# The split weights of an encoder trunk moved to other byte offsets

## The chip, the core and the metric

The kernel runs on one core of one Trainium2 chip. The time is device microseconds of one execution; the median of three runs is given, and one more execution was recorded by the hardware profiler. TensorE (PE in the profile) multiplies, with its weight loads shown as an engine of their own (PEld); VectorE is DVE, ScalarE ACT, GpSimd POOL, and SyncE (SP) issues most DMAs.

## What is computed

Two layers of an encoder on 256 tokens of width 1024, in float32, and a last RMSNorm:

```
def hybrid_layer(x, ...):
    h = rms_norm(x, g_mix)
    b_a, c_a, x_a, u_p, q, k, v, ga, gp, gt = jnp.split(h @ w_in, split_points(), axis=-1)
    y_a = short_conv_mixer(b_a, c_a, x_a, conv_w, w_a_out)
    y_p = multiscale_pool_mixer(u_p, w_pool, pool_scale)
    y_t = windowed_gqa(q, k, v, rel_bias, sink) @ w_attn_out
    merged = sigmoid(ga) * y_a + sigmoid(gp) * y_p + sigmoid(gt) * y_t
    x = x + merged @ w_o
    gate, up = jnp.split(rms_norm(x, g_ffn) @ w_gu, [D_FF], axis=-1)
    return x + (silu(gate) * up) @ w_down
```

The weights of both layers are read once, about 170 MB; each 128x128 block of them is used for all 256 tokens.

## The kernel before

Activations lie with channels on the 128 partitions and tokens along the free dimension. Every float32 product is made of three reduced-precision ones: a value is split into a high part (`hi` for weights, the first half of a pair for activations) and a remainder (`lo`, the second half). `mm3` issues the three matmuls of a block: high weight by high activation (L166), high weight by low activation (L167), low weight by high activation (L168). Each has a 128x128 block of weights as the stationary operand, which a weight load brings in, and 256 columns of an activation as the moving one. The only products with the operands the other way round are those of the last layer's down projection (`down_nat`, L626 to L628): there the activation `fa` is stationary and 512 columns of weights stream.

`plan_layer` writes out the order in which blocks are used, and the host lays the blocks out in that order in `wst`. A chunk of 16 blocks (1 MB) is one DMA into one of three `raw` tiles. `convert` splits half a chunk, 8 blocks: ScalarE casts it to `hi` (L139) and VectorE subtracts (`lo`, L140). `advance`, called from `take` whenever a half chunk is begun, converts three half chunks ahead. `hi` and `lo` are tags with five buffers each in the pool `wp`, so the sixth half chunk overwrites the first.

Beside these blocks TensorE computes the attention scores (`sc`, L356 and L357, stationary `q`, moving `kk`), transposes the probabilities (`pt`, L385), multiplies them with the values (`o`, L400, stationary `vt`), and sums squares for the norms. `norm_rows` and the transposes of `x` (`xt`, L684) are a few matmuls more.

Pools place their tiles one after another in each partition. The constants come first, then `wp`, then `act`, which begins with the tile `x`, then `tmp`. The tile `x` holds 96 numbers of parameters and 112 unused ones ahead of the activations:

```
NG = L * 6 * KT + 112
xc = act.tile([P, NG + KT * T], F32, name="x")
```

All tiles that hold split activations are 2048 bytes long and follow each other (`xg`, `z` and `m`; `q`, `ao` and `fa`; `h`; `pp`), and both halves of a pair are 1024 bytes, so that all begin at one place within 512 bytes. The same holds for the blocks in `hi` and `lo`.

Of the kernel before, what the change touches and what calls it, by code (L numbers as in the profile page):

```python
# [9 lines left out]
F32R = mybir.dt.float32r  # L10
# [6 lines left out]
P = 128  # L17
# [7 lines left out]
NEG = -1e30  # L25
CB, CC, CX, CU, CQ, CK, CV, CGA, CGP, CGT = 0, 8, 16, 24, 32, 40, 42, 44, 52, 60
CT = 16
HT = 8

HEADS = []  # L30
# [5 lines left out]
def plan_layer(last):  # L36

    out = []

    def inner(mat, ns, nk=KT):  # L40
        for n in ns:
            for k in range(nk):
                out.append((mat, k, n))

    def outer(mat, ns, nk=KT):
        for k in range(nk):
            for n in ns:
                out.append((mat, k, n))

    outer("in", (CK, CK + 1, CV, CV + 1))  # L50
    for q in range(2):
        inner("in", [CQ + 4 * q + j for j in range(4)])
    inner("in", [CGA + n for n in range(8)])
    for n in range(8):
        inner("in", (CC + n, CX + n, CB + n))
    inner("in", (CU, CU + 1))
    inner("a", range(8))
    for n in range(8):
        inner("in", (CGP + n, CGT + n))
        if n % 2 == 1 and n < 7:  # L60
            inner("in", (CU + n + 1, CU + n + 2))
        inner("t", (n,))
        out.extend(("pool", k, n) for k in range(2))
        if n >= 2:
            out.extend(("o", n - 2, m) for m in range(8))
    for j in range(4):
        out.extend(("o", k, m) for k in (6, 7) for m in (2 * j, 2 * j + 1))
    for q in range(NQ):
        ns = (2 * q, 2 * q + 1, FT + 2 * q, FT + 2 * q + 1)
        if q == 0:  # L70
            outer("gu", ns)
        else:
            inner("gu", ns)
        if q >= 1:
            for k in (2 * q - 2, 2 * q - 1):
                out.extend(("down", k, m) for m in range(8))
    ks = (2 * NQ - 2, 2 * NQ - 1)
    if last:
        for k in ks:
            out.extend(("down", k, m) for m in range(8))  # L80
    else:
        for j in range(4):
            out.extend(("down", k, m) for k in ks for m in (2 * j, 2 * j + 1))
    return out


NCH = len(plan_layer(False)) * L // CT

# [4 lines left out]
def trunk(ctx, tc, wst, xT, sinkb, rb, invc, gfin, ident_d, out):  # L93
# [5 lines left out]
    wp = ctx.enter_context(tc.tile_pool(name="wp", bufs=3))  # L99
# [2 lines left out]
    psA = ctx.enter_context(tc.tile_pool(name="psA", bufs=4, space=PSUM))  # L102
    psB = ctx.enter_context(tc.tile_pool(name="psB", bufs=4, space=PSUM))

    uid = [0]

    def nm(s):
# [10 lines left out]
    def dma_chunk(c):  # L118
        raw = wp.tile([P, CT * P], F32, name=f"raw{c}", tag="raw", bufs=3)
        if c < 2:  # L120
            for a, b, xa, xb in (((0, 4, 0, 1), (4, 8, 1, 2), (8, 16, 2, 4)), ((0, 8, 4, 6), (8, 16, 6, 8)))[c]:
                s = slice(0 if xa == 0 else NG + xa * T, NG + xb * T)
                if xa == 0:
                    nc.sync.dma_start(xc[:, s], xT[:, s])
                nc.sync.dma_start(raw[:, a * P:b * P], wst[c, :, a * P:b * P])
                if xa > 0:
                    nc.sync.dma_start(xc[:, s], xT[:, s])
        else:
            nc.sync.dma_start(raw, wst[c])
        raws[c] = raw  # L130

    def convert(hc):
        c = hc // 2
        raw = raws[c][:, (hc % 2) * HT * P:(hc % 2 + 1) * HT * P]
        hi = wp.tile([P, HT * P], F32R, name=f"hi{hc}", tag="hi", bufs=5)
        lo = wp.tile([P, HT * P], F32R, name=f"lo{hc}", tag="lo", bufs=5)
        for a, b in (((0, 4), (4, 8)) if hc < 2 else ((0, 8),)):
            s = slice(a * P, b * P)
            S.activation(hi[:, s], raw[:, s], AF.Copy)  # L139
            V.tensor_tensor(lo[:, s], raw[:, s], hi[:, s].bitcast(F32), op=ALU.subtract)  # L140
        his[hc], los[hc] = hi, lo

    def advance(pos):
        while state["dma"] < NCH and state["dma"] * CT <= pos + 3 * CT - 1:
            dma_chunk(state["dma"])
            state["dma"] += 1
        while state["cv"] < 2 * NCH and state["cv"] * HT <= pos + 3 * HT:
            convert(state["cv"])
            state["cv"] += 1

    def take(key, width=1):
        pos = state["pos"]
        if pos % HT == 0:
            advance(pos)
        for i in range(width):
            l, mat, k, n = plan[pos + i]
            assert (l, mat, k, n) == (key[0], key[1], key[2], key[3] + i), (plan[pos + i], key)
        hc, j = pos // HT, pos % HT
        assert j + width <= HT
# [544 lines left out]
    for j in range(4):  # L704
        convert(j)
        xg_tiles(0, 0, j, st)
# [141 lines left out]
```

## Time and profile before

| | |
|---|---|
| median of 3 runs | 960.26 us (959.83 to 961.04) |
| the profiled execution | 965.28 us |
| its span, first to last instruction | 963.1 us |
| granted TensorE clock | 0.999 |
| matmuls, weight loads | 7881, 7881 |
| moved by DMA | 178.17 MB, mean 185 GB/s |

The span is what the profile shows; some 2 us of the execution lie outside it. Busy time of TensorE adds up overlapping matmuls only once, so a busy share near 100% tells that it never stood still, not how fast it went. The views used below are the page's list of engines and its chain of work, the groups by line (count, busy us, mean ns of one, idle time ahead of them), the timeline of one engine (start, duration) and the table of stretches.

### The profile page before, as it was taken

Reading aid. Unit: us, or ns where it says so; the run is one execution under the profiler, and the core shown is the slowest. Engines: PE = TensorE matmul, PEld = TensorE weight load, DVE = VectorE, ACT = ScalarE, POOL = GpSimd, SP = SyncE. Lnnn points to the kernel's source line nnn. Section 1 sums busy time; section 2 is a strip of 40 time slices with the busy share of each in tenths; the row PEclk is TensorE's granted clock in tenths of the full one; section 3 lists DMA queues with packets and bytes.
Section 4 is the critical chain, followed back from the end, with each engine's and each line's share of the span. In section 5 each row is a group of like instructions: output and inputs, shape, how many; then the busy total and the mean of one; then the engine's idle time right before and its main releaser. Section 6 shows DMA issues by size and latency. Waiting matters only on the chain.

```text
span 963.1 us, 19117 instructions
## 1 busy us (share of the span) xinstructions
PE 952.8 (99%) x7881; PEld 939.9 (98%) x7881; DVE 711.3 (74%) x1277; ACT 551.0 (57%) x916; POOL 38.8 (4%) x60
## 2 busy tenths in 40 slices
PE   8999999999999999999999999999999999999997
PEld 8999999999999999999999999999999999999996
DVE  7999998577679955545599998975677698555555
ACT  6866777655456644444477666765545575444444
POOL 5000000000001000000020000000000020000000
PEclk9999999999999999999999999999999999999999
DMA  8656545544554555555543745444555455655541
GB/s 300 251 186 210 202 162 173 198 176 176 203 191 174 178 190 200 179 177 194 197 178 132 246 166 185 148 171 175 181 197 192 176 190 182 218 176 187 197 142 44
DMA packets 26967, 178.17 MB, mean 185 GB/s; under 512 B 3136, under 2 KB 3664, under 8 KB 6656
## 3 DMA queue, kind: packets, MB, share of 16 engines
q1 hardware_dynamic: 24768, 169.99, 49.8%
q0 software_dynamic: 2112, 6.97, 2.5%
q8 instruction: 61, 1.00, 0.4%
q14 instruction: 26, 0.21, 0.1%
HBM read 175.86 MB, written 1.08 MB: 184 GB/s over the span
## 4 chain that ended last, share of the span: by engine, by line
PE 98%; DMA 1%; DVE 0%; ACT 0%; SPq 0%; issue 0%
PE b L167 25%; PE b L166 25%; PE b L168 25%; PE dn L166 2%; PE dn L168 2%; PE dn L167 2%; PE dn L628 2%; PE dn L627 2%; PE dn L626 2%; PE wo L167 2%; PE wo L166 2%; PE o L400 2%; PE wo L168 2%; PE pt L385 1%; PE sc L357 1%; PE sc L356 1%
## 5 line engine op out<-in xcount | busy, mean ns | idle before, releaser
L140 DVE TENSOR_TENSOR lo<-raw,hi 128x1024 fp32r<-128x1024 f32 (+1 forms) x322 | 389.5, 1218 | 200.9 <-ACT hi L139 199.9
L139 ACT ACTIVATE hi<-raw 128x1024 fp32r<-128x1024 f32 (+1 forms) x322 | 335.9, 1051 | 308.4 <-PE b L167 189.7
L166 PE MATMUL b<-h,hi 128*128 128x256 f32 x1344 | 377.4, 281 | 0.0
L168 PE MATMUL b<-h,lo 128*128 128x256 f32 x1344 | 376.0, 280 | 0.0
L167 PE MATMUL b<-h,hi 128*128 128x256 f32 x1344 | 376.0, 280 | 0.0
L166 PEld LDWEIGHTS b<-h,hi 128*128 128x128 f32 x1344 | 255.0, 190 | 0.2
L168 PEld LDWEIGHTS b<-h,lo 128*128 128x128 f32 x1344 | 253.9, 189 | 0.0
L167 PEld LDWEIGHTS b<-h,hi 128*128 128x128 f32 x1344 | 252.4, 188 | 0.2
L166 PE MATMUL b<-xg,hi 128*128 128x256 f32 x448 | 125.2, 280 | 0.9 <-DVE xg L253 0.9
L167 PE MATMUL b<-xg,hi 128*128 128x256 f32 x448 | 124.9, 279 | 0.9 <-DVE xg L256 0.9
L168 PE MATMUL b<-xg,lo 128*128 128x256 f32 x448 | 124.7, 278 | 0.2 <-DVE lo L140 0.2
L167 PEld LDWEIGHTS b<-xg,hi 128*128 128x128 f32 x448 | 84.2, 188 | 1.3 <-DVE xg L256 1.3
L166 PEld LDWEIGHTS b<-xg,hi 128*128 128x128 f32 x448 | 84.2, 188 | 1.1 <-ACT hi L139 1.0
L168 PEld LDWEIGHTS b<-xg,lo 128*128 128x128 f32 x448 | 84.6, 189 | 0.4 <-DVE lo L140 0.4
L166 PE MATMUL dn<-fa,hi 128*128 128x256 f32 x176 | 49.5, 281 | 0.0
L167 PE MATMUL dn<-fa,hi 128*128 128x256 f32 x176 | 49.5, 281 | 0.0
L168 PE MATMUL dn<-fa,lo 128*128 128x256 f32 x176 | 49.5, 281 | 0.0
L369 ACT ACTIVATE s<-s,sm 128x256 f32<-128x256 f32 x64 | 31.7, 497 | 17.5 <-DVE sm L364 17.5
L166 PE MATMUL b<-z,hi 128*128 128x256 f32 x128 | 36.3, 284 | 0.0
L168 PE MATMUL b<-z,lo 128*128 128x256 f32 x128 | 36.0, 281 | 0.0
L166 PE MATMUL b<-ao,hi 128*128 128x256 f32 x128 | 36.0, 281 | 0.0
L167 PE MATMUL b<-ao,hi 128*128 128x256 f32 x128 | 36.0, 281 | 0.0
(176 smaller groups left out, 1494.1 us busy)
## 6 DMA issues: line engine op xcount, KB each, us to landing
raw<-wst SPq DMA_DIRECT2D x158, 1024.0 KB, 4.9
bias<-stab POOLq DMA_DIRECT2D x16, 384.0 KB, 4.5
raw<-wst SPq DMA_DIRECT2D x3, 512.0 KB, 8.0
out<-yg SPq DMA_DIRECT2D x4, 256.0 KB, 2.2
x<-xT SPq DMA_DIRECT2D x3, 256.0 KB, 8.0
raw<-wst SPq DMA_DIRECT2D x2, 256.0 KB, 5.1
gf<-gfin POOLq DMA_DIRECT2D x2, 256.0 KB, 3.1
x<-xT SPq DMA_DIRECT2D x1, 232.0 KB, 2.7
```

The costliest lines, as they stand in the source:

```text
L139: S.activation(hi[:, s], raw[:, s], AF.Copy)
L140: V.tensor_tensor(lo[:, s], raw[:, s], hi[:, s].bitcast(F32), op=ALU.subtract)
L166: PE.matmul(dst, wh, xh, start=start, stop=False, skip_group_check=skip)
L167: PE.matmul(dst, wh, xl, start=False, stop=False, skip_group_check=skip)
L168: last_mm[0] = PE.matmul(dst, wl, xh, start=False, stop=stop, skip_group_check=skip)
L356: PE.matmul(ps[:, half(j)], qs[t][j][:, cs], kh, start=True, stop=False)
L357: PE.matmul(ps[:, half(j)], qs[t][j][:, cs], kl, start=False, stop=True)
L369: S.activation(ss[i // 2][:, i % 2], ss[i // 2][:, i % 2], AF.Exp, bias=sm[:, 4 + i:5 + i], accum_out=sm[:, 12 + i:13 + i])
L400: PE.matmul(ps[:, half(j)], vv, pts[kt][i][:, half(j)], start=(kt == i == 0), stop=(kt == i == 1))
L626: PE.matmul(d, ah[:, cs], wh, start=(k == 0), stop=False)
L627: PE.matmul(d, ah[:, cs], wl, start=False, stop=False)
L628: PE.matmul(d, al[:, cs], wh, start=False, stop=(k == FT - 1))
```

## The change

The ten buffers `hi` and `lo` become slices of one tile, `split_w`. A slot is 4096 bytes as before, five for `hi` and then five for `lo`, reused in the same rotation; the first begins 5 elements, or 20 bytes, into the tile. The tile has 8 elements, or 32 bytes, more than the ten slots need.

```
 CT = 16
+HB, WOFF = 5, 5
 HT = 8
...
+    split_w = wp.tile([P, 2 * HB * HT * P + 8], F32R, name="split_w", bufs=1)
...
     raw = raws[c][:, (hc % 2) * HT * P:(hc % 2 + 1) * HT * P]
-    hi = wp.tile([P, HT * P], F32R, name=f"hi{hc}", tag="hi", bufs=5)
-    lo = wp.tile([P, HT * P], F32R, name=f"lo{hc}", tag="lo", bufs=5)
+    hi, lo = [split_w[:, i + WOFF:i + WOFF + HT * P]
+              for i in (hc % HB * HT * P, (HB + hc % HB) * HT * P)]
```

The two programs have the same instructions in the same order on every engine, with the same waits. They differ in addresses. In bytes within a partition, modulo 512:

| | before | changed |
|---|---|---|
| `raw` | 224 | 256 |
| split weights | 224 | 244 |
| split activations | 160 | 192 |
| weights minus activations, 7,152 matmuls (L166 to L168) | 64 | 52 |
| the same for 264 matmuls with the operands exchanged (L626 to L628) | 448 | 460 |
| `q` minus `kk`, scores (L356, L357) | 128 | 128 |
| `vt` minus probabilities (L400) | 0 | 0 |
| probabilities minus `ident`, transposes (L385) | 320 | 352 |

In each row with a minus, the stationary operand's place stands first and the moving one's is taken off. `raw` now lies behind the split weights, since the one tile is allocated first.

## The prediction

> **What bounds the kernel.** I read the page first: busy time, then the chain that ended last.
>
> ```profile
> PE 952.8 (99%) x7881; PEld 939.9 (98%) x7881; DVE 711.3 (74%) x1277; ACT 551.0 (57%) x916; POOL 38.8 (4%) x60
> PE 98%; DMA 1%; DVE 0%; ACT 0%; SPq 0%; issue 0%
> ```
>
> TensorE holds 98% of the chain. So what counts is the step from the start of one matmul to the start of the next, which no view prints: the duration of one matmul, some 0.28 us, overlaps the next two. I take the step from the timeline of TensorE, where the first column is the start in microseconds, at two places.
>
> ```profile
> 499.73 0.28 PE L168 MATMUL b<-xg,lo 128*128 128x256 f32 x1
> 499.84 0.28 PE L166 MATMUL b<-xg,hi 128*128 128x256 f32 x1
> ...
> 501.43 0.28 PE L168 MATMUL b<-xg,lo 128*128 128x256 f32 x1
> 399.76 0.28 PE L167 MATMUL b<-h,hi 128*128 128x256 f32 x1
> 399.88 0.28 PE L168 MATMUL b<-h,lo 128*128 128x256 f32 x1
> ...
> 401.41 0.28 PE L166 MATMUL b<-h,hi 128*128 128x256 f32 x1
> ```
>
> From 499.73 to 501.43 lie 15 steps: 113.3 ns each. From 399.76 to 401.41 lie 14: 117.9 ns. These are the same instructions, 256 columns against a split weight tile, with the same places of operands within 512 bytes, and neither piece has an idle TensorE. **There are two paces, and they last.** The table of stretches shows how long (us, then busy time and matmuls of each engine, granted clock in the column after POOL):
>
> ```profile
> 33.00:57.00 24.00, 24.00 (x214) 24.00 (x213) 23.37 (x49) 18.81 (x35) 0.00 (x0) 1.00 0.38 134
> 180.00:291.00 111.00, 111.00 (x945) 111.00 (x944) 75.86 (x125) 58.56 (x82) 0.00 (x0) 1.00 0.52 181
> 311.50:494.00 182.50, 182.50 (x1552) 182.50 (x1552) 116.49 (x142) 88.84 (x119) 5.67 (x4) 1.00 0.52 183
> 507.00:531.00 24.00, 24.00 (x214) 24.00 (x213) 23.44 (x48) 17.50 (x32) 0.00 (x0) 1.00 0.39 133
> ```
>
> A row also counts the two or three matmuls that cross its edges, about 2.4. So 24.00 / 211.6 = 113.4 ns in the first and last, and 182.50 / 1549.6 = 117.8 ns in the third. The clock is 1.00 in all four, so it isn't the throttle. How many matmuls go at each pace can be read from their durations, which differ too (the groups of 34 to 56 us, then of 182 to 290 us, then of the whole run):
>
> ```profile
> L167 PE MATMUL b<-xg,hi 128*128 128x256 f32 x65 | 17.9, 276 | 0.0
> L167 PE MATMUL b<-h,hi 128*128 128x256 f32 x176 | 49.5, 281 | 0.0
> L167 PE MATMUL b<-h,hi 128*128 128x256 f32 x1344 | 376.0, 280 | 0.0
> L168 PE MATMUL b<-xg,lo 128*128 128x256 f32 x448 | 124.7, 278 | 0.2 <-DVE lo L140 0.2
> ```
>
> Fast is 276 ns, slow 281 ns. 376.0 us / 1344 = 279.8 ns, so a quarter of the h matmuls are fast; 124.7 / 448 = 278.3 ns, so half of the xg matmuls are; z, ao, m and fa stand at 281. That makes 4032 / 4 + 1344 / 2, about 1,700 of 7,152. Counting the starts of all 7,152 one by one gives 1,841 steps of 112 to 115 ns, 5,231 of 116 to 119 ns, and 80 beside a wait or a change of operand. I use these.
>
> **The change, part by part.** The number, order, waits and sizes of instructions stay, and so do 10 slots of 1024 weights with the same reuse. What changes is where bytes lie. (1) The split weights begin at byte 244 of 512 instead of 224. (2) Everything allocated behind them moves up by 32 bytes, so the activations begin at 192 instead of 160. (3) The distance from activation to weight becomes 52 bytes instead of 64 for the 7,152 matmuls, and 460 instead of 448 for the 264 of 512 columns. (4) Distances that don't involve the split weights stay: 128 for the scores, 0 for the value products. What (1) to (3) do to the pace is the whole question, and this trace holds distances 64, 448, 128 and 0 only. Rows of the last two, and of the shortest step in the trace, the transposes (the row of the chain gives 8 in 0.87 us):
>
> ```profile
> 83.15 0.28 PE L356 MATMUL sc<-kk,q 128*128 128x256 f32 x1
> ...
> 84.11 0.27 PE L385 MATMUL pt<-ident,s 128*128 128x128 f32 x1
> 76.54 0.28 PE L400 MATMUL o<-ph,vt 128*128 128x256 f32 x1
> ...
> 77.50 0.28 PE L166 MATMUL b<-h,hi 128*128 128x256 f32 x1
> 70.36 0.87 PE pt L385 x8
> ```
>
> Eight steps each: 0.96 / 8 = 120 ns at distance 128, 0.96 / 8 = 120 ns at distance 0, and 0.87 / 8 = 109 ns for a transpose, which streams half the columns and takes a whole weight load, so that the load is likely to pace it. So 109 ns is the nearest thing to a **floor**, distances 0 and 128 cost 11 ns over it, and distance 64 costs 4.5 or 9. The good place lies between 0 and 128, and 52 is inside. That is the argument for a gain. It is not a proof, since a straight line from 0 to 64 would put 52 about 0.4 to 1.3 ns above the two paces of 64.
>
> Terms, against the profiled execution (965.28 us, of which 963.1 are span; the median of three is 960.26, half a per cent less, so I take differences):
> - Slow steps that become fast: 5,231 x (117.8 - 113.35) = 23.3 us. If instead fast ones become slow: 1,841 x 4.45 = 8.2 us lost.
> - 264 matmuls of 512 columns. From 810.40 to 811.54 in the timeline lie five steps:
>
> ```profile
> 810.40 0.39 PE L626 MATMUL dn<-hi,fa 128*128 128x512 f32 x1
> ...
> 811.54 0.39 PE L628 MATMUL dn<-hi,fa 128*128 128x512 f32 x1
> ```
>
> That is 228 ns, 10 over twice the 109; at distance 460 anything from -10 to +10 ns, so -2.6 to +2.6 us. I take 0, since the place moves least in proportion.
> - Writes of the split weights that start off a 32-byte boundary. VectorE has such a pair in the convolution:
>
> ```profile
> L506 DVE SCALAR_TENSOR_TENSOR y<-c,x,y 128x255 f32<-128x255 f32 x16 | 7.7, 480 | 1.7 <-ACT y L505 1.2
> L507 DVE SCALAR_TENSOR_TENSOR y<-c,x,y 128x255 f32<-128x255 f32 x16 | 7.7, 478 | 0.1
> L139 ACT ACTIVATE hi<-raw 128x1024 fp32r<-128x1024 f32 x318 | 333.5, 1057 | 302.8 <-PE b L167 189.7 <-PE dn L167 30.4 <-PE dn L628 26.9
> ```
>
> L506 writes 4 bytes in, L507 at the tile's start: 480 and 478 ns, so nothing. For ScalarE no row shows it. It may lose or gain; its 318 casts of 1057 ns have 302.8 us of idle time ahead of them, most of it waiting for TensorE to free a slot, and that time is the cover. Only if each became over half longer would the attention stretches run out of it. I take 0.
> - What is late next if TensorE speeds up: VectorE, busy 23.37 of 24.00 us in the first stretch above, and 23.44 of 24.00 in the last. Both are fast already, so the forecast isn't capped; at 109 ns the same 211 matmuls take 23.1 us, and VectorE would hold each stretch back by about 0.3 us.
>
> Sum: 960.26 - 23.3 = **937 us**.
>
> The Trainium skill, "TensorE: Matmul & The Clock Gate", Part 2, step 1, says that TensorE reads the streamed operand and the weights through two independent ports, so that a weight load takes no read bandwidth from the running matmul. By that rule the place of one against the other changes nothing, and the sum is 960; the paces of 113.4, 117.8 and 120 ns for one shape at one clock don't rule it out, but leave nothing else in sight that differs.
>
> **The rivals.**
> - *Slower: the load gets longer.* In the slow stretch one weight load in three takes longer than the others, in the fast one none does (groups of 182 to 290, then of 34 to 56 us):
>
> ```profile
> L166 PEld LDWEIGHTS b<-h,hi 128*128 128x128 f32 x176 | 33.8, 192 | 0.0
> L167 PEld LDWEIGHTS b<-h,hi 128*128 128x128 f32 x176 | 33.0, 188 | 0.0
> L166 PEld LDWEIGHTS b<-xg,hi 128*128 128x128 f32 x65 | 12.2, 188 | 0.0
> ```
>
> A slot that begins 20 bytes in no longer starts on a 32-byte boundary. If that adds 4 ns to a load, and the load's end starts the next matmul, the fast pace becomes about 117.4 and nothing else gains: all 7,072 steps near 117.8, 960.26 + 8.2 = 968. It decides from the point where a load is longer than the 113.4 ns step leaves room for. For it: fast and slow differ by one such 4 ns. Against: the long load may be an effect of the slow pace. The Trainium skill, "SBUF — State Buffer", the note on cachelines, says that memory is read in 16-byte lines and that each crossing into a new one pays a penalty; 512 bytes that start 4 bytes into a line touch 33 of them instead of 32. No run here shows a load at such a place.
> - *Slower, toward distance 0.* If 52 behaves as 0 does, all go to 120 ns: 5,231 x 2.2 + 1,841 x 6.65 = 23.8 us, 984. For it: it's a step in that direction. Against: 52 is nearer to 64.
> - *Faster still.* If the two streams no longer meet at all, the steps reach the 109 ns: 5,231 x 8.8 + 1,841 x 4.35 = 54 us, 906. For it: the transposes show that a load can follow a load every 109 ns. Against: no 256-column matmul in the trace runs so.
> - *Nothing.* If the distance isn't what sets the pace (a pace that was only picked up at a wait or at a transpose would be the same whatever the place), both paces stay in their shares: 960. Against: steps at 0 and 128 are slower from their first to their last.
>
> **How the numbers follow.** Nearly all steps at the fast pace, 930 to 945: 0.36, the likeliest, because the fast pace is one that this kernel already holds for 24 us on end and 52 stays inside the good side. Partly so, 945 to 958: 0.08. Toward the floor, below 930: 0.20, a quarter of it below 905. No change, within 0.2% (which is about what a measurement of this kernel can tell): 0.08. All slow or a longer load, 963 to 970: 0.16. Toward 120 ns, above 970: 0.12, a third of it above 980. Faster 0.64, same 0.08, slower 0.28. The range of 905 to 976 leaves out about 0.13: 0.05 below and 0.08 above. The likeliest case's own range is 930 to 945.
>
> **What would show it.** If I am right, the stretches from 180 to 291 and from 311 to 494 us hold the same matmuls in about 107 and 176 us, with durations of 276 and no load of 192 ns. If the load is the cause, L166's load groups stand at 192 everywhere and the stretch from 33 to 57 grows to 25 us. If the floor is reached, VectorE's waits begin to stand ahead of TensorE between 33 and 57. Wrong altogether would be a wait of TensorE for ScalarE's cast, since nothing that I costed makes one.

## The result and the profile after

The changed kernel takes 949.95 us (median of 4 runs, 948.51 to 950.22) where the kernel before took 960.05 us in the same set (959.53 to 961.04): a ratio of 0.9891, with a 95% interval of 0.9873 to 0.9908. The forecast was 937. The way was right, and so was the means, slow steps that become fast. The size was not: 10.1 us instead of 23.3. The two profiled executions lie further apart than the medians, 965.28 and 948.51 us, with spans of 963.1 and 946.4.

The page of the changed kernel: engines, the chain of work that ended last, then the groups that answer to those of before (line, engine, operation; count; busy us, mean ns of one; idle time ahead). L166 to L168 are now L170 to L172.

```profile
PE 936.4 (99%) x7881; PEld 922.0 (97%) x7881; DVE 711.2 (75%) x1277; ACT 551.1 (58%) x916; POOL 38.1 (4%) x60
PE 93%; DVE 3%; DMA 2%; ACT 1%; issue 1%; SPq 0%; DVEq 0%
L144 DVE TENSOR_TENSOR split_w<-raw,split_w 128x1024 fp32r<-128x1024 f32 (+1 forms) x322 | 389.8, 1220 | 186.3 <-ACT split_w L143 186.0
L143 ACT ACTIVATE split_w<-raw 128x1024 fp32r<-128x1024 f32 (+1 forms) x322 | 336.6, 1053 | 293.0 <-PE b L171 178.7
L171 PE MATMUL b<-h,split_w 128*128 128x256 f32 x1344 | 371.9, 277 | 0.0
L170 PEld LDWEIGHTS b<-h,split_w 128*128 128x128 f32 x1344 | 252.5, 188 | 0.2
L171 PE MATMUL b<-xg,split_w 128*128 128x256 f32 x448 | 125.0, 279 | 0.9 <-DVE xg L260 0.9
```

The h matmuls have gone from 280 to 277 ns, so nearly all of them are fast (276); the xg matmuls have not moved. The casts and subtractions that write to the new offset take 1053 and 1220 ns, where the page of before has 1051 and 1218. The mean weight load is not longer: 188 ns. The chain runs over TensorE for 93%, where it was 98%, since in the first 60 us it now passes over two transfers, ScalarE and VectorE. There VectorE was nearly full before as well (23.37 of 24.00 us from 33 to 57 us). TensorE's waits in the profile add up to 2.6 us, and before to 3.2, so no time went that way. The table of stretches shows the paces by counts:

```profile
33.00:57.00 24.00, 24.00 (x213) 24.00 (x213) 23.35 (x49) 18.81 (x34) 0.00 (x0) 1.00 0.37 137
180.00:286.00 106.00, 106.00 (x937) 106.00 (x936) 75.09 (x124) 57.51 (x81) 0.00 (x0) 1.00 0.53 189
308.00:482.00 174.00, 174.00 (x1538) 174.00 (x1536) 114.26 (x141) 88.64 (x117) 5.68 (x4) 1.00 0.53 189
500.00:524.00 24.00, 24.00 (x206) 24.00 (x206) 23.62 (x45) 15.40 (x25) 0.00 (x0) 1.00 0.49 178
```

With 2.4 matmuls taken off for the edges, the second and third stretch go at 106.00 / 934.6 = 113.4 and 174.00 / 1535.6 = 113.3 ns, where the kernel before had 117.8. That is the forecast gain. But the last, which was all fast before with 214 matmuls, now has 206. And the timeline of TensorE in the attention of the first layer shows the same (start and duration in us):

```profile
143.72 0.28 PE L172 MATMUL b<-h,split_w 128*128 128x256 f32 x1
...
145.16 0.28 PE L172 MATMUL b<-h,split_w 128*128 128x256 f32 x1
```

Twelve steps in 1.44 us: 120 ns. The kernel before, at this place:

```profile
143.69 0.28 PE L167 MATMUL b<-h,hi 128*128 128x256 f32 x1
...
145.16 0.28 PE L168 MATMUL b<-h,lo 128*128 128x256 f32 x1
```

Thirteen steps in 1.47 us: 113 ns. So distance 52 has a slow pace of its own, 120 ns, and takes it in places that were fast before.

### The profile page after: what moved, and what is told of

Read it like the earlier page. It is cut to its first block, busy times and chain, and to the rows that moved or that the text cites. A ratio compares the mean times of both kernels' runs of the same rounds, so it can differ in the third digit from the quotient of the medians.

```text
span 946.4 us, 19117 instructions
## 1 busy us (share of the span) xinstructions
PE 936.4 (99%) x7881; PEld 922.0 (97%) x7881; DVE 711.2 (75%) x1277; ACT 551.1 (58%) x916; POOL 38.1 (4%) x60
## 4 chain that ended last, share of the span: by engine, by line
PE 93%; DVE 3%; DMA 2%; ACT 1%; issue 1%; SPq 0%; DVEq 0%
PE b L171 24%; PE b L172 23%; PE b L170 23%; PE dn L630 2%; PE dn L632 2%; PE dn L631 2%; PE dn L171 2%; PE dn L172 2%; PE dn L170 2%; PE o L404 2%; PE wo L170 2%; PE wo L171 2%; PE wo L172 2%; DMA raw<-wst 2%; PE pt L389 1%; DVE split_w L144 1%
## 5 line engine op out<-in xcount | busy, mean ns | idle before, releaser
L144 DVE TENSOR_TENSOR split_w<-raw,split_w 128x1024 fp32r<-128x1024 f32 (+1 forms) x322 | 389.8, 1220 | 186.3 <-ACT split_w L143 186.0
L143 ACT ACTIVATE split_w<-raw 128x1024 fp32r<-128x1024 f32 (+1 forms) x322 | 336.6, 1053 | 293.0 <-PE b L171 178.7
L170 PE MATMUL b<-h,split_w 128*128 128x256 f32 x1344 | 373.5, 278 | 0.0
L172 PE MATMUL b<-h,split_w 128*128 128x256 f32 x1344 | 372.0, 277 | 0.0
L171 PE MATMUL b<-h,split_w 128*128 128x256 f32 x1344 | 371.9, 277 | 0.0
L171 PEld LDWEIGHTS b<-h,split_w 128*128 128x128 f32 x1344 | 252.8, 188 | 0.2
L170 PEld LDWEIGHTS b<-h,split_w 128*128 128x128 f32 x1344 | 252.5, 188 | 0.2
L172 PEld LDWEIGHTS b<-h,split_w 128*128 128x128 f32 x1344 | 252.4, 188 | 0.0
L171 PE MATMUL b<-xg,split_w 128*128 128x256 f32 x448 | 125.0, 279 | 0.9 <-DVE xg L260 0.9
L170 PE MATMUL b<-xg,split_w 128*128 128x256 f32 x448 | 124.8, 279 | 0.3 <-DVE xg L257 0.3
L172 PE MATMUL b<-xg,split_w 128*128 128x256 f32 x448 | 124.6, 278 | 0.3 <-DVE split_w L144 0.2
L171 PEld LDWEIGHTS b<-xg,split_w 128*128 128x128 f32 x448 | 84.3, 188 | 1.3 <-DVE xg L260 1.3
L172 PEld LDWEIGHTS b<-xg,split_w 128*128 128x128 f32 x448 | 84.1, 188 | 0.8 <-DVE split_w L144 0.8
L170 PEld LDWEIGHTS b<-xg,split_w 128*128 128x128 f32 x448 | 84.2, 188 | 0.6 <-ACT split_w L143 0.5
L172 PE MATMUL dn<-fa,split_w 128*128 128x256 f32 x176 | 48.6, 276 | 0.0
L170 PE MATMUL dn<-fa,split_w 128*128 128x256 f32 x176 | 48.6, 276 | 0.0
L171 PE MATMUL dn<-fa,split_w 128*128 128x256 f32 x176 | 48.6, 276 | 0.0
L170 PE MATMUL b<-z,split_w 128*128 128x256 f32 x128 | 35.9, 280 | 0.0
L172 PE MATMUL b<-z,split_w 128*128 128x256 f32 x128 | 35.5, 278 | 0.0
L171 PE MATMUL b<-z,split_w 128*128 128x256 f32 x128 | 35.5, 278 | 0.0
L170 PE MATMUL b<-ao,split_w 128*128 128x256 f32 x128 | 35.3, 276 | 0.0
```

The costliest lines, as they stand in the source:

```text
L170: PE.matmul(dst, wh, xh, start=start, stop=False, skip_group_check=skip)
L171: PE.matmul(dst, wh, xl, start=False, stop=False, skip_group_check=skip)
L172: last_mm[0] = PE.matmul(dst, wl, xh, start=False, stop=stop, skip_group_check=skip)
```

## The experiments

All offsets below were reached by two numbers, the first offset `WOFF` and what the tile holds beyond its slots, which moves the activations. "Step" is the time from one matmul's start to the next one's.

**The kernel before, once more.** No edit.

> The kernel before, unchanged, to see how much of the 16.8 us between the two profiled spans is the one execution that was profiled (965.28 us against a median of 960). If the share of slow steps differs from one execution to the next: a profiled time near 960, some 1,000 fewer of the 117.8 ns steps than the 5,231, and the stretches that are slow or fast not all the same. If it is fixed: 5,231 again, and the time differs by something other than the pace.

959.82 us (0.9999 of before, 0.998 to 1.0019). The profiled execution has 959.69 us and a span of 956.4 us, 6.8 less than the first one (956.35 against 963.15), with the same program. Counted one by one it has 3,759 steps of 116 to 119 ns instead of 5,231, and 3,315 of 112 to 115 instead of 1,841. The stretches show where:

```profile
180.00:291.00 111.00, 111.00 (x945) 111.00 (x944) 75.87 (x125) 58.59 (x82) 0.00 (x0) 1.00 0.52 181
312.50:487.00 174.50, 174.50 (x1542) 174.50 (x1542) 114.84 (x142) 88.61 (x117) 5.69 (x4) 1.00 0.53 188
```

From 180 us the 945 matmuls are slow again. But the first layer's FFN, 1,550 matmuls from 312 us, went at 174.50 / 1539.6 = 113.3 ns. In the execution on which the prediction rests it went at 117.8. 1,550 x 4.45 ns are 6.9 us, about the whole difference of the spans; some 80 other steps went the other way. Most executions of this kernel fall near 960 us or near 966, as one stretch's 6.9 us would have it, though only two were profiled. How many fall near 966 changes from set to set: 3 of 31 were above 964 us in this set, and 20 of 29 in a later one, on another chip.

**Distance against place.** Distance 64 with the activations at 192, then distance 52 with the activations back at 160.

```
-HB, WOFF = 5, 5
+HB, WOFF = 5, 8
```

```
-HB, WOFF = 5, 5
+HB, WOFF = 5, 125
...
-    split_w = wp.tile([P, 2 * HB * HT * P + 8], F32R, name="split_w", bufs=1)
+    split_w = wp.tile([P, 2 * HB * HT * P + 128], F32R, name="split_w", bufs=1)
```

> The weights at distance 64 as before, all else as in the changed kernel: activations at 192, weights at 256, one tile. If the distance sets the pace: like before, steps of 113.3 and 117.8 ns, most of them slow, 960 us. If it is the place of the activations (192, on a 64-byte boundary, instead of 160): like the changed kernel, about 6,200 fast steps, 950 us.

> Distance 52 with the activations back at 160 and the weights at 212, one tile. If the distance sets the pace: like the changed kernel, about 6,200 steps of 113.4 ns, the rest in groups of 118, 121 and 121, 950 us. If the place of the activations does: like before, 960 us.

d64_a192: 963.91 us (ratio 1.0026, 1.0001 to 1.0051), steps of 113.35 and 117.77 ns, of the latter 4,760. d52_a160: 952.26 us (0.9916, 0.989 to 0.9943), steps of 113.35 ns, and 1,414 of 116 to 124, which in the longer slow pieces come in turns of about 118, 122 and 120 ns (the expectations have 118, 121 and 121). Each has the paces of its distance, not of its place, and d64_a192 has the one tile of the changed kernel too, so the tile isn't the cause either. Nor is the place of the weights alone: at distances 44 and 76 in the table below they begin at the same byte, 236, and the times are 973 and 945 us. The long stretches of d64_a192, then of d52_a160:

```profile
181.00:290.00 109.00, 109.00 (x928) 109.00 (x927) 74.23 (x124) 56.72 (x79) 0.00 (x0) 1.00 0.52 184
312.50:492.00 179.50, 179.50 (x1526) 179.50 (x1526) 113.67 (x141) 87.36 (x116) 5.65 (x4) 1.00 0.51 181
```

```profile
185.00:287.00 102.00, 102.00 (x903) 102.00 (x902) 72.62 (x120) 53.82 (x75) 0.00 (x0) 1.00 0.54 193
311.00:485.00 174.00, 174.00 (x1537) 174.00 (x1537) 114.38 (x140) 88.48 (x117) 5.66 (x4) 1.00 0.54 188
```

**Other distances.** One number changes in each (`WOFF`; the tile as in one of the two above).

> Distance 44: one step of 8 bytes more on the way from 64 to 52, activations at 192. If a shorter distance is better all the way: more than 6,213 fast steps, or a pace below 113.3, under 950 us. If the good place is a narrow one, as the straight line between distances 0 and 64 has it: slower than the changed kernel, toward 120 ns, above 955 us.

> Distance 48, between 44 (973 us, slow states of 117.7 and 120 ns) and 52 (950 us). If the good place is narrow and begins between 44 and 52: either like 52 (950) or like 44 (973), nothing smooth between. If the cost falls evenly with distance: about 961.

> Distance 56, between 52 and 64. If the states belong to a few bytes of distance each: it keeps either the slow state of 52 (118, 121, 121 ns) or that of 64 (117.8 ns); with that of 52 and a wide catch of the fast one 950 us or less, with that of 64 about 960.

> Distance 60: as for 56, one step nearer to 64. By distance alone between 950 and 960 us; a pace below 113.3 ns would be new, and would take it under 943, which is where all steps at 113.3 ns end.

> Distance 72, the other side of 64, activations at 160. If 64 is at the edge of the good side and 52 further in: slower than before, over 963 us. If the cost of a distance is even about 64: like 56.

> Distance 40. The two good distances so far, 52 and 64, are 12 bytes apart, with 56 and 60 slower than both. If the good places repeat every 12 bytes, 40 is another: under 960 us, long runs at 113.3 ns. If 52 stands alone on this side: slow, 970 to 985 us, as 44 and 48.

> Distance 76, 12 bytes on the other side of 64. If the good places repeat every 12 bytes: under 960 us, long runs at 113.3 ns. Otherwise slow, about 978 as 72.

> Distance 116, which is 52 and 64 more. If what matters is the distance within 64 bytes: the same paces as the changed kernel, 950 us. If it is the distance within a longer period, such as the 512 in the words of the change: something else, and by the 120 ns at distance 128 slower than before.

> Distance 88, the next in the row 52, 64, 76, which were good where 40 was not. If the row goes on: long runs at 113.3 ns, 945 to 960 us. If it ends: slow, 970 to 985 us.

The last two columns are counted from the starts of one profiled execution each: the mean step from 320 to 480 us (the first layer's FFN), and how many of 7,152 steps are of 112 to 115 ns. Each ratio is to the kernel before in the same set, whose median was between 959.94 and 965.70 us.

| distance | median us | ratio to before (95%) | step, ns | fast steps |
|---|---|---|---|---|
| 40 | 984.39 | 1.0228 (1.0187 to 1.0268) | 119.2 | 4 |
| 44 | 973.28 | 1.013 (1.0098 to 1.0162) | 117.8 | 1,150 |
| 48 | 979.77 | 1.0192 (1.0151 to 1.0233) | 117.8 | 9 |
| 52, the change | 949.95 | 0.9891 (0.9873 to 0.9908) | 113.3 | 6,213 |
| 56 | 973.48 | 1.013 (1.0097 to 1.0162) | 117.8 | 1,196 |
| 60 | 984.20 | 1.024 (1.0208 to 1.0273) | 119.5 | 539 |
| 64, before | 960.05 | 1 | 117.8 or 113.3 | 1,841 and 3,315 |
| 72 | 978.44 | 1.0179 (1.014 to 1.0218) | 118.3 | 1,267 |
| 76 | 945.27 | 0.9847 (0.9778 to 0.9916) | 113.3 | 6,742 |
| 88 | 962.05 | 0.9966 (0.9939 to 0.9992) | 116.7 | 2,155 |
| 116 | 981.33 | 1.0198 (1.0157 to 1.0238) | 119.0 | 5 |

Nothing in this is smooth. 52, 64 and 76 are good, 12 bytes apart; 88 is about as before, with a slow pace of 116.7 ns; 40, 44, 48, 56, 60, 72 and 116 are 1.3 to 2.4% slower than before. 56 and 60, expected at 960 us or less, came out at 973 and 984, and 88 fell between its two expected ranges; the others went by one of the cases named for them. 116, which is 52 and one 64 more, has nothing of 52, so it isn't the distance within 64 bytes that counts. A longer period than 64 was not tried. At the seven slow distances never more than two steps in a row are of 112 to 115 ns: what the last column counts there are single steps of a mixed sequence. At 88 there are runs of up to 212.

**The changed kernel, once more.** No edit.

> The changed kernel once more, for the profile of a second execution: are its 890 steps of 118 to 121 ns in the same stretches (behind the transposes of the attention, 60 to 150 us, and 495 to 520 us), and as many. If they come with the place: 800 to 950 again in the attention stretches, and the long stretches fast, 949 to 950 us. If they come by chance as in the kernel before: another count, and a span that differs by 4 to 7 ns for each.

950.33 us (0.9871, 0.9824 to 0.9918), profiled execution 951.73 us with a span of 949.6. It has 1,256 steps of 116 to 124 ns, more than expected, against 890 in the first.

```profile
42.00:57.00 15.00, 14.82 (x123) 14.82 (x124) 14.76 (x29) 9.93 (x19) 0.00 (x0) 1.00 0.57 211
180.00:286.00 106.00, 106.00 (x937) 106.00 (x936) 73.59 (x121) 57.96 (x82) 0.00 (x0) 1.00 0.55 192
312.00:485.00 173.00, 173.00 (x1529) 173.00 (x1528) 113.36 (x140) 88.62 (x117) 5.67 (x4) 1.00 0.54 189
```

In the first attention (71 to 180 us) it has 317 of them where the first execution had 351, and from 495 to 523 us 138 where that had 153. A further 231 stand from 42 to 71 us, which the first had fast but for 5 steps, and a run of 121 at 291 us, where it was fast as well. The two long stretches are fast in both. So in these two executions part of the slow pieces came back and part did not: the pace of a piece isn't fixed by the program.

**A disturbance in the long stretch.** Four transposes that nobody reads, behind four blocks of the first layer's FFN, in the kernel before and in the changed one. The attention has such transposes, this FFN has none.

```
+            if not last and q in (2, 4, 6, 8):
+                ps = newB("xt")
+                for i in range(4):
+                    PE.transpose(ps[:, i * P:(i + 1) * P], x[:, i, :P], ident)
```

> The kernel before with four transposes of x, whose result nobody reads, put in behind the second, fourth, sixth and eighth block of four tiles of the first layer's FFN: 16 more matmuls, 1.7 us of steps and four switches of about 0.1 us. Distance 64. If the pace is a state that is carried from matmul to matmul and picked anew at a disturbance: the stretch of 1,550 matmuls, which went at 117.8 ns from end to end in one execution and at 113.3 in another, falls into pieces of about 300, and both paces stand in one execution. If something else sets the pace of that stretch (what it computes, another engine's work): one pace from end to end.

> The changed kernel with the same four disturbances in the first layer's FFN. Distance 52. In its two profiles that stretch was fast from end to end. If each disturbance gives the slow state (118, 121, 121 ns) a chance, as the transposes of the attention do: some pieces of up to 300 matmuls at a mean of 120 ns, up to 2 us each. If the fast state catches it whatever comes: a few slow steps behind each, then 113.3 ns.

break_before took 962.74 us (0.9982, 0.9956 to 1.0008). Its five pieces:

```profile
313.00:343.00 30.00, 30.00 (x257) 30.00 (x256) 26.74 (x43) 17.00 (x28) 0.00 (x0) 1.00 0.54 195
344.50:377.50 33.00, 33.00 (x283) 33.00 (x282) 18.62 (x20) 13.91 (x18) 0.00 (x0) 1.00 0.51 189
379.50:411.00 31.50, 31.50 (x280) 31.50 (x280) 18.07 (x20) 13.93 (x18) 0.00 (x0) 1.00 0.54 195
412.50:444.00 31.50, 31.50 (x280) 31.50 (x279) 18.17 (x20) 13.89 (x17) 0.00 (x0) 1.00 0.55 196
445.50:493.00 47.50, 47.50 (x422) 47.50 (x421) 33.12 (x39) 25.97 (x35) 5.65 (x4) 1.00 0.49 175
```

30.00 / 254.6 and 33.00 / 280.6 are 117.8 and 117.6 ns, 31.50 / 277.6 (twice) and 47.50 / 419.6 are 113.5 and 113.2. One stretch of equal work, two paces, and the change stands at the second disturbance, at 377.7 us. break_after took 957.33 us (0.993, 0.9905 to 0.9955), with three pieces at 113.3 ns and two at 120:

```profile
339.50:370.50 31.00, 31.00 (x276) 31.00 (x276) 17.57 (x20) 13.88 (x17) 0.00 (x0) 1.00 0.53 193
373.00:406.00 33.00, 33.00 (x278) 33.00 (x277) 17.42 (x19) 14.38 (x18) 0.00 (x0) 1.00 0.49 176
443.00:492.00 49.00, 49.00 (x411) 49.00 (x410) 33.97 (x40) 26.07 (x36) 5.63 (x4) 1.00 0.45 164
```

31.00 / 273.6 is 113.3 ns, 33.00 / 275.6 and 49.00 / 408.6 are 119.7 and 119.9. Each change stands at one of the four disturbances, and the pace is then kept for up to 400 matmuls, as it would be if the pace were a state carried from matmul to matmul. Each of the two kernels was profiled once.

**Distance 76 at the other place.** `WOFF = 11`, the tile 136 elements longer than its slots.

> Distance 76, the best so far, with the activations at 192 instead of 160. If the distance alone sets the states: 113.3 ns in over 6,500 steps as at 160, 944 to 947 us, faster than the changed kernel. If the two good results at 76 and 52 owe something to the place too: another mix.

951.82 us (0.9868, 0.9818 to 0.9918): three runs of 944.6 to 947.1 and three of 956.6 to 957.8. The profiled one is of the latter:

```profile
181.00:285.00 104.00, 104.00 (x920) 104.00 (x919) 73.74 (x122) 55.66 (x77) 0.00 (x0) 1.00 0.54 192
312.00:492.00 180.00, 180.00 (x1502) 180.00 (x1501) 110.99 (x131) 85.00 (x112) 5.64 (x4) 1.00 0.51 177
```

Here the FFN has taken the slow pace of 76, 180.00 / 1499.6 = 120.0 ns. It lasts for 1,556 steps from 305 us, and 1,556 x 6.67 = 10.4 us is about what lies between the two groups of runs. All loads of this stretch last 188 ns, so this slow pace has no longer load. One of the four runs at 160 was 956.58 as well. So the expectation of 944 to 947 held in half of the executions. Distance 76 has the fastest executions found: at 160 it took 943.8 to 945.9 us in three runs of four, beside 949.6 to 951.7 for the changed kernel in the same set. But in the others it gives 10 us back: the mean of its ten runs at both places is 950.0 us, and that of the changed kernel's eight is 950.1.

## Why the prediction was right in its way and wrong in its size

- *What bounds the kernel, and two paces that last:* right. The paces were the whole matter: both programs have the same instructions and waits, casts and subtractions kept their durations, and TensorE waited no longer (2.6 us in all, before 3.2).
- *Slow steps that become fast, at 113.35 ns:* right for the two stretches that the prediction named. They go at 113.3 to 113.4 ns, with 276 ns a matmul and no load of 192. By their starts, the same 943 and 1,550 steps took 111.1 and 182.6 us before and take 106.9 and 175.7; 107 and 176 were forecast.
- *The term 5,231 x 4.45 ns = 23.3 us, taken as a difference and set against the median:* **this step failed first.** The count came from an execution of 965.28 us, and the median was 960.26. The prediction saw that half per cent and took differences, as if it had nothing to do with the pace. It was the pace: 1,550 of the slow steps were one stretch that went fast in the other execution that was profiled, at 959.69 us. From its 3,759 slow steps the term is 3,759 x 4.43 = 16.7 us.
- *Nearly all steps at the fast pace:* **this failed second.** The likeliest case has no slow steps left, and gives no reason why the new distance should have no slow pace of its own. It has one, of 120 ns: 890 steps in one execution and 1,256 in the other were slow. In the first 457 of them were 7.25 ns over the fast pace and 433 were 4.6 over it, 5.3 us; in the second 693 were 7.2 over it and 563 were 4.8 over it, 7.7 us. Many of these steps were fast before, as at 143.7 us.
- *The 264 matmuls of 512 columns, taken as 0 within 2.6 us:* 229.8 ns became 233.7, 1.0 us lost, inside the bound.
- With these the sum closes. Between the first profiles: 5,231 x 4.43 = 23.2, and 23.2 - 5.3 - 1.0 = 16.9 us; the spans, 963.15 and 946.37, differ by 16.8. From the second execution of before, which is near the median: 16.7 less 5.3 to 7.7 and 1.0 leaves 8.0 to 10.4 us, and 10.1 were measured.
- *The argument that the good place lies between 0 and 128 and 52 is inside, with a straight line as the caution:* the line is refuted. 40, 44, 48, 56, 60, 72 and 116 lie between 0 and 128 too and are 1.3 to 2.4% slower than before. That 52 gained was luck: of the ten distances tried beside 64 seven lost, and nothing in the trace of before could tell 52 from 56.
- *The rivals:* the longer load fell, since loads last 188 ns on average with slots that start 4 bytes into a 16-byte line. The penalty for crossing into a new line, in the note on cachelines of the Trainium skill, "SBUF — State Buffer", has no visible price here. The load of 192 ns went with the slow pace of 64 in the two stretches named, and the slow pace of 76 does without one, so it is not what makes a pace slow. "Nothing" fell as well: eleven distances, with the same instructions, took 945 to 984 us. That speaks against reading "TensorE: Matmul & The Clock Gate", Part 2, step 1, of the Trainium skill as saying that the place of the two operands doesn't matter; it doesn't show that a port is shared, only that the place sets the pace. The floor of 109 ns was not reached at any distance: no stretch of the 7,152 matmuls went below 113.3. Nor was 109 the shortest step of the trace, as the prediction has it, but the shortest that a run of transposes keeps up; single steps of 28 ns stand behind transposes.

What stays open is why the distance acts as it does, and which condition at a disturbance decides the pace that follows it.

## What to carry to other kernels

Where TensorE never stands still, read the step from one matmul's start to the next, stretch by stretch: equal work at several paces means that something other than the work sets part of the time. Here it was the distance between two addresses, and, at one distance, the execution. Sweep the offset between stationary and moving operands in steps of one element, since neighbours of a good offset can be the worst, and run each candidate often enough to see its slower executions. And before a profile's count becomes a saving, look whether the profiled execution is a typical one: half a per cent between it and the median was here a whole stretch that went at the other pace.

## What was not expected of the hardware

The paces keep to a beat. The long stretches at distances 52, 64, 76 and 88 have four mean steps between them, 113.33 (at 52, 64 and 76), 116.67 (at 88), 117.78 (at 64) and 120.00 ns (at 76). These are 17, 17.5, 17.67 and 18 times 6.667 ns. Taking each start modulo this beat (20/3 ns exactly, for the rounding would add up), for every third matmul, gives in the first profile of the kernel before:

```
stretch, us   starts modulo 6.667 ns, three matmuls in turn
 33 to 57     4.0  3.7  4.3     (113.3 ns)
297 to 307    3.7  3.3  4.0     (113.3 ns)
800 to 810    3.0  2.7  3.3     (113.3 ns)
182 to 222    3.0  0.5  5.5     (117.8 ns)
655 to 700    4.7  2.3  6.3     (117.8 ns)
```

All stretches at 113.3 ns start their matmuls at one point of the beat, which drifts by about a nanosecond in 800 us whatever lies between; this holds for each of the 23 runs of 30 or more fast steps in this profile. Those at 117.8 ns visit three points in turn, a third of the beat apart. The other distances keep to the beat too: from 330 to 470 us the starts at distances 116, 40 and 60 repeat, to about a nanosecond, after 7, 8 and 13 matmuls, which are 125, 143 and 233 beats. The starts of VectorE's 1277 instructions spread over the beat (31, 36 and 33% in its three thirds), so the beat doesn't come from the recording as a whole. A matmul's step seems to depend on where in the beat it starts, which would make a pace that repeats itself until something moves it. That is argued and not shown; what beats so was not tried.
